# Changing the order of the mixer's input projections in a two-layer hybrid encoder

## The chip, the core and the metric

The kernel runs on one NeuronCore of a Trainium2 chip. Five engines take part: TensorE (PE in the profile, with its weight loads as PEld) multiplies 128x128 tiles into PSUM, VectorE (DVE) and ScalarE (ACT) work on tiles, GpSimd (POOL) does a little arithmetic and issues some transfers, and SyncE (SP) issues the rest. Each engine runs its own list of instructions in a fixed order; semaphores make an instruction wait for what it needs from another engine. The metric is the time of one execution on the device in microseconds, median of several runs; lower is better.

## What is computed

The model has two layers on 512 tokens of width 1024, all in float32. The change touches the first half of a layer, the mixer. One projection of the normalized input makes the gate z, the streams x, B, C of the state-space heads, their step sizes, and the queries, keys and values of the attention heads:

```python
h = rms_norm(x, norm1_w[i])
proj = h @ w_in[i]
z, xbc, dt_raw, q, k, v = jnp.split(proj, [Z_END, XBC_END, DT_END, Q_END, K_END], axis=-1)
xbc = jax.nn.silu(depthwise_conv_centered(xbc, conv_w[i], conv_b[i]))   # 7 taps
xs, bm, cm = jnp.split(xbc, [SSM_WIDTH, SSM_WIDTH + BC_WIDTH], axis=-1)
...
y_fwd = ssd_chunked(xs, dt[:, :, 0], a[0], bm, cm)      # 4 chunks of 128, 2 groups of 8 heads
y_bwd = flip(ssd_chunked(flip(xs), flip(dt[:, :, 1]), a[1], flip(bm), flip(cm)))
y_ssm = y_fwd + y_bwd + d_skip[i][:, None] * xs
y_ssm = rms_norm(y_ssm * silu(z), ssm_norm_w[i])         # per group
y_attn = windowed_gqa(q, k, v, attn_sink[i], band_bias)  # 16 heads, 4 key heads, window 128
x = x + concat([y_ssm, y_attn]) @ w_out[i]
...
x = x + (silu(conv3(g)) * u) @ w_down[i]                 # the FFN half, not touched
```

The attention needs q, k and v. The state-space part of a group needs that group's B, C and x after convolution and Silu, and the gate z only at its end.

## The kernel before

**Dense products.** Every weight and activation is split in a high part and a rest, and a product is three matmuls (`mm3`, L263 to L265): high x high, high x rest, rest x high. Weights come in units of 512 KB, loaded by SyncE into `raw`; ScalarE makes the high part `whi` (L155) and VectorE the rest `wlo` (L156). Units are used in the order in which they are listed (L164 to L193); three split units and three raw ones are held. A projection of 256 columns by `g_ws` (L442) is two such units and two steps (a `yield` after each) of 24 matmuls of 512 columns; the gate projection `g_z` (L738) is four steps of 48 matmuls of 256 columns; the output projection `g_out` (L926) is six steps of 24 matmuls for each half.

**Work beside the dense products.** `Side` (L365) holds a list of smaller steps. `side.run(gen, rate)` goes through the steps of a projection, and after each lets `rate` small steps follow (a credit, at most 2). So rates say how many small steps stand beside one dense step. What is listed here is the order in which the program is written; a scheduler then moves instructions a little within each engine's list.

**The small steps.** Attention has 16 items for a layer, one for each key head and block of 128 queries: scores (`attn_scores`, L551: TensorE L564 and L565 into four small PSUM banks, which VectorE frees by L566; Exp on ScalarE L580), transposes (L598) and values (L608), two items later each. The state-space part (`ssd_steps`, L761) has 14 small steps for a group. For each of eight pieces u (4 chunks, two halves of the heads) `build` makes the weights `dd` (ScalarE L815, VectorE L816) and `decay` the factor `em` (VectorE L826 and L830, Exp on ScalarE L831, VectorE L832), which `inner` multiplies on TensorE (L841). `states` (L778: VectorE L783, TensorE L788, VectorE L790) and `outer` (L851: TensorE L858, VectorE L860 to L863) do the rest; the last one multiplies by the gate `sz`. Then come a scale (L869) and the transposes of the result (L878).

**B, C and x.** After their projection a block of 2 x 128 channels goes through `conv` (L352): one ScalarE instruction (L354) and six taps on VectorE (L360) for each 128 channels, then Silu (L682). Transposes on TensorE follow (L694, L729), written after the next projection so that TensorE need not wait for the Silu.

**The order.** In a layer the program is written thus: values and step sizes, keys, queries of key head 0; queries 1 to 3, then B/C, x (two blocks) and z of group 0, with attention's 19 steps beside them; then B/C, x and z of group 1 with the state-space steps of group 0; then the two output halves with the rest of group 0 and those of group 1. Behind that, `mixT` (L913 to L920) splits the attention result (ScalarE L918, VectorE L919), which is the first operand of the output projection.

**Storage.** Nine 8 KB buffers (`act_tile`) hold the split input hT (4), the keys (2), then x and z of the groups, and later the split attention result and the mixer's result. There are four dense PSUM banks (`psd`) and four small ones (`pss`).

Of the kernel before, what the change touches and what calls it, by code (L numbers as in the profile page):

```python
# [14 lines left out]
P = 128  # L15
# [9 lines left out]
X0 = 1024  # L25
# [16 lines left out]
RATE_Q = 1.3  # L42
RATE_XBC = 0.8
RATE_Z = 0.9
RATE_S0 = 1.2
RATE_S1 = 1.3
# [3 lines left out]
def encoder_kernel(  # L50
# [113 lines left out]
    for i in range(DEPTH):  # L164
# [9 lines left out]
        for g in range(NKV):  # L174
            pair(f"q{g}", [(Q0 + 256 * g, 256)])
        for g in range(GROUPS):
            pair(f"bc{g}", [(B0 + P * g, P), (C0 + P * g, P)])
            pair(f"xa{g}", [(X0 + 512 * g, 256)])
            pair(f"xb{g}", [(X0 + 512 * g + 256, 256)])
            for half in range(2):  # L180
                pair(f"z{g}{half}", [(512 * g + 256 * half, 256)])
# [255 lines left out]
    for i in range(DEPTH):  # L437
        side = Side()
        with ExitStack() as mix:
# [230 lines left out]
            side.run(g_q(0), 0)  # L670
            for g in range(1, NKV):
                side.run(g_q(g), RATE_Q)
            side.steps += [lambda: attn_push(None)] * (LAG + 1)


            def g_xbc(g, r):
# [7 lines left out]
                def bc_done(banks):  # L684
                    bT = ep.tile([P, L], F32, tag="xT", name=nm("bT"), bufs=2)
                    cT = ep.tile([P, L], F32, tag="cT", name=nm("cT"), bufs=2)
                    stage(banks, (8 + g, 10 + g), (bT, cT))
                    r.update(bT=bT, cT=cT)

# [23 lines left out]
                yield from g_ws((i, f"bc{g}"), hT, bc_done)  # L713
                xk = act_tile(F32)
                r["xk"] = xk
                turns = [bc_turn]

                def x_done(b, banks):
                    for t in turns:
                        t()  # L720
                    turns.clear()
# [12 lines left out]
                for b, nme in enumerate(("xa", "xb")):  # L734
                    yield from g_ws((i, f"{nme}{g}"), hT, lambda banks, b=b: x_done(b, banks))
                r["turns"] = turns

            def g_z(g, r):  # L738
                sz = act_tile(F32)
                r["sz"] = sz  # L740
                for half in range(2):
                    ws = [take((i, f"z{g}{half}", j)) for j in range(2)]
                    cs = slice(256 * half, 256 * half + 256)
                    for tp in range(2):
# [8 lines left out]
                        if half == 0 and tp == 0:  # L753
                            for turn in r["turns"]:
                                turn()
# [5 lines left out]
            def ssd_steps(sp, g, r):  # L761

                h0 = GH * g
                xk, bk, cT, cbf, cbb, sz = (r[k] for k in ("xk", "bk", "cT", "cbf", "cbb", "sz"))
# [86 lines left out]
                def outer(c):  # L851
# [10 lines left out]
                    V.tensor_tensor(y, y, pys[c], ALU.add)  # L862
                    V.tensor_tensor(sz[:, c], sz[:, c], y, ALU.mult)  # L863
                    S.activation(y, sz[:, c], AF.Square, accum_out=ss[:, c : c + 1])

                def scale():
                    rs = rstd_of(ss, 512, NT)
                    for c in range(NT):
                        S.mul(sz[:, c], sz[:, c], rs[:, c : c + 1])  # L869
                    mixS[g] = (act_tile(), act_tile())  # L870

                def turn(js):
                    oh_, ol_ = mixS[g]
                    for j in js:
# [28 lines left out]
            side.run(g_xbc(0, r0), RATE_XBC)  # L903
            side.run(g_z(0, r0), RATE_Z)
# [6 lines left out]
            side.run(g_xbc(1, r1), RATE_S0)  # L911
            side.run(g_z(1, r1), RATE_S0)
# [31 lines left out]
            for half in range(2):  # L944
                side.run(g_out(half), RATE_S1)
# [127 lines left out]
```

## Time and profile before

| | |
|---|---|
| time, median of 3 runs | 1590.67 us (1590.48 to 1591.53) |
| time of the profiled execution | 1591.11 us |
| span from the first to the last instruction in it | 1589.4 us |
| mean granted TensorE clock, as a share of full speed | 0.983 |
| TensorE busy | 1529.4 us, 96% of the span |
| weight loads busy | 1248.3 us, 79% |
| VectorE busy | 935.4 us, 59% |
| ScalarE busy | 774.0 us, 49% |
| GpSimd busy | 183.6 us, 12% |

The profiled execution took 0.44 us more than the median, of which 1.7 us lie outside the span. A busy TensorE is not one at its best: matmuls overlap, so their number and the distance from one start to the next say how much work a stretch holds, and what the stretch takes beyond that is lost. Busy shares over the whole span say little here, since a layer has stages with different limits; the two layers are alike, about 780 us apart.

### The profile page before, as it was taken

The page shows a single profiled execution, that of the slowest core. Times are in us where ns is not written, and L with a number is a line of the kernel's source. Part 1 is how long each engine was busy: PE and PEld are TensorE (multiplying, and loading weights), DVE is VectorE, ACT ScalarE, POOL GpSimd, SP SyncE. Part 2 cuts the span into 40 slices and gives each one's busy share as a digit, 9 for nine tenths or more (in the row PEclk, how much of TensorE's full clock was granted, in tenths as well). Part 3 has the DMA queues.
Part 4 walks back from the last instruction along what each step waited for, and adds up shares of the span by engine and source line. Part 5 has one row for each costly group of instructions (what it writes and reads, how often), then busy time and mean ns, then how long its engine had stood idle before and what let it go on. Part 6 is the DMA issues. An engine that isn't in the chain of part 4 may idle for free.

```text
span 1589.4 us, 20122 instructions
## 1 busy us (share of the span) xinstructions
PE 1529.4 (96%) x7676; PEld 1248.3 (79%) x7676; DVE 935.4 (59%) x1494; ACT 774.0 (49%) x1372; POOL 183.6 (12%) x226
## 2 busy tenths in 40 slices
PE   5999999799999999999999999997999999999997
PEld 5877878577788888888887788785778888888886
DVE  3677759997554444433366685799965444443333
ACT  4387885743443333322356779765435323332223
POOL 4000012323200000000010000223322000000002
PEclk9999999799999999999999999997999999999999
DMA  8423233453133333222343322445531332233221
GB/s 247 132 74 85 76 93 94 119 160 93 66 107 106 93 93 105 94 93 93 96 133 101 93 62 60 125 94 145 134 106 60 100 106 93 93 98 101 93 93 66
DMA packets 113796, 162.00 MB, mean 102 GB/s; under 512 B 8010, under 2 KB 90186, under 8 KB 113692
## 3 DMA queue, kind: packets, MB, share of 16 engines
q1 hardware_dynamic: 105476, 133.12, 27.1%
q0 software_dynamic: 7648, 27.50, 7.3%
q8 instruction: 60, 0.98, 0.3%
q14 instruction: 36, 0.29, 0.1%
q10 hardware_dynamic: 576, 0.10, 0.0%
HBM read 156.34 MB, written 8.55 MB: 104 GB/s over the span
## 4 chain that ended last, share of the span: by engine, by line
PE 85%; DVE 7%; ACT 3%; issue 2%; POOL 1%; DMA 1%; POOLq 0%; ACTq 0%; DVEq 0%
PE pd L265 21%; PE pd L263 21%; PE pd L264 21%; PE psm L263 3%; PE psm L264 3%; PE psm L265 3%; PE psm L608 2%; PE psm L598 2%; DVE wlo L156 2%; PE psm L841 2%; PE psm L564 1%; ACT whi L155 1%; PE psm L858 1%; PE psm L565 1%; DVE dd L816 1%
## 5 line engine op out<-in xcount | busy, mean ns | idle before, releaser
L156 DVE TENSOR_TENSOR wlo<-raw,whi 128x1024 fp32r<-128x1024 f32 (+1 forms) x230 | 283.9, 1237 | 279.7 <-ACT whi L155 279.0
L263 PE MATMUL pd<-t,whi 128*128 128x512 f32 (+1 forms) x1088 | 419.6, 386 | 0.0
L265 PE MATMUL pd<-t,wlo 128*128 128x512 f32 (+1 forms) x1088 | 418.5, 385 | 0.4 <-DVE wlo L156 0.4
L264 PE MATMUL pd<-t,whi 128*128 128x512 f32 (+1 forms) x1088 | 417.5, 384 | 0.0
L155 ACT CAST whi<-raw 128x1024 fp32r<-128x1024 f32 (+1 forms) x230 | 238.5, 1041 | 268.7 <-PE pd L264 212.7
L265 PEld LDWEIGHTS pd<-t,wlo 128*128 128x128 f32 x1088 | 204.4, 188 | 41.9 <-DVE wlo L156 1.6
L263 PEld LDWEIGHTS pd<-t,whi 128*128 128x128 f32 x1088 | 204.1, 188 | 40.4 <-issue 2.2
L264 PEld LDWEIGHTS pd<-t,whi 128*128 128x128 f32 x1088 | 204.4, 188 | 39.2 <-issue 1.0
L263 PE MATMUL pd<-whi,t 128*128 128x256 f32 (+2 forms) x544 | 188.7, 347 | 0.6 <-ACT t L756 0.3
L265 PE MATMUL pd<-whi,t 128*128 128x256 f32 (+2 forms) x544 | 183.2, 339 | 2.8 <-DVE t L919 2.8
L264 PE MATMUL pd<-wlo,t 128*128 128x256 f32 (+2 forms) x544 | 182.3, 335 | 0.1
L265 PEld LDWEIGHTS pd<-whi,t 128*128 128x128 f32 x544 | 105.0, 194 | 15.4 <-DVE t L919 5.9
L263 PEld LDWEIGHTS pd<-whi,t 128*128 128x128 f32 x544 | 105.0, 193 | 13.9 <-issue 2.0
L264 PEld LDWEIGHTS pd<-wlo,t 128*128 128x128 f32 x544 | 104.8, 193 | 12.0 <-issue 2.9
L1016 DVE TENSOR_TENSOR pl<-t,ph 128x512 fp32r<-128x512 f32 x40 | 27.7, 692 | 119.4 <-ACT ph L1015 119.4
L1015 ACT CAST ph<-t 128x512 fp32r<-128x512 f32 x40 | 24.8, 620 | 147.7 <-PE psm L264 137.2
L566 DVE CUSTOM_DVE_ANT_0 s<-psm,bias,sink_all 128x256 f32<-128x256 f32 (+1 forms) x128 | 65.9, 547 | 31.4 <-PE psm L565 17.7
L360 DVE SCALAR_TENSOR_TENSOR sg<-pd,fprm,sg 128x511 f32<-128x511 f32 x88 | 65.8, 748 | 30.7 <-ACT sg L354 29.0
L580 ACT ACTIVATE s<-s,nm 128x257 f32<-128x257 f32 (+1 forms) x128 | 70.6, 554 | 13.8 <-DVE nm L577 13.5
L263 PE MATMUL pd<-whi,ph 128*128 128x512 f32 x176 | 69.7, 396 | 0.0
L264 PE MATMUL pd<-wlo,ph 128*128 128x512 f32 x176 | 69.6, 396 | 0.0
L265 PE MATMUL pd<-whi,pl 128*128 128x512 f32 x176 | 69.5, 395 | 0.0
(185 smaller groups left out, 2207.5 us busy)
## 6 DMA issues: line engine op xcount, KB each, us to landing
raw<-in_w_up_dram SPq DMA_DIRECT2D x88, 512.0 KB, 3.5
raw<-in_w_in_dram SPq DMA_DIRECT2D x52, 512.0 KB, 4.1
raw<-in_w_down_dram SPq DMA_DIRECT2D x44, 512.0 KB, 3.5
rows<-sums POOLq DMA_DIRECT2D x32, 512.0 KB, 5.6
raw<-in_w_out_dram SPq DMA_DIRECT2D x32, 512.0 KB, 3.7
bias<-toep POOLq DMA_DIRECT2D x16, 384.0 KB, 4.1
raw<-in_w_in_dram SPq DMA_DIRECT2D x18, 256.0 KB, 3.4
toep<-table POOLq DMA_DIRECT2D x4, 1024.0 KB, 9.4
```

The lines of the kernel that those rows point to most:

```text
L155: S.copy(hi[:, :used], raw[:, :used])
L156: V.tensor_tensor(lo[:, :used], raw[:, :used], f(hi[:, :used]), ALU.subtract)
L263: mm(o, lh, rh, start=start, stop=False)
L264: mm(o, lh, rl, start=False, stop=False)
L265: mm(o, ll, rh, start=False, stop=stop)
L360: V.scalar_tensor_tensor(dst[:, lo:hi], src[:, lo + d : hi + d], taps[k], dst[:, lo:hi], ALU.mult, ALU.add)
L566: V.tensor_tensor_reduce(out=s4[:, h, :w], in0=ps[:, :w], in1=it.bias[h // 2][:, h % 2, it.j0 : it.j1], scale=1.0, scalar=sink4[:, h : h + 1],
L580: S.activation(s4[:, h, : w + 1], s4[:, h, : w + 1], AF.Exp, bias=nm4[:, h : h + 1], accum_out=den[:, h : h + 1])
L598: turn128(ps[:, c : c + P], it.s4[:, h, b * P : (b + 1) * P], ident)
L608: mm(po[c * HD : (c + 1) * HD, :256], v_sb[:, it.k0 // P + b, it.g * HD : (it.g + 1) * HD], it.pts[b][:, c * 256 : (c + 1) * 256], start=( ...
L841: mm(pys[c][:, hc : hc + HD], ems[u][:, h * P : (h + 1) * P], xk[:, c, hc : hc + HD], start=True, stop=True,)
L1016: V.tensor_tensor(l, p_sb[kt], f(h), ALU.subtract)
```

## The change

The list of weight units and the program's order are changed; no operation is added or removed in the program. Group 0's B/C come before the queries; the two x blocks of group 0, B/C of group 1 and both x blocks of group 1 alternate with queries 1 to 3, and all of them but the first two projections run beside attention (rate 1.2). Both gates z now run beside the state-space steps of group 0, before the output projection (rate 1.4 for all of these). The transposes of a convolved block are kept in one list, `turns`, and written after the next projection of B, C, x or z. The state-space steps look up the gate `sz` when they need it, since it is made beside them.

```diff
-RATE_Q = 1.3
-RATE_XBC = 0.8
-RATE_Z = 0.9
-RATE_S0 = 1.2
-RATE_S1 = 1.3
+RATE_A = 1.2
+RATE_S = 1.4
...
         pair("k", [(K0, 256)])
-        for g in range(NKV):
-            pair(f"q{g}", [(Q0 + 256 * g, 256)])
+        for nme in ("bc0", "q0", "xa0", "q1", "xb0", "q2", "bc1", "q3", "xa1", "xb1"):
+            g = int(nme[-1])
...
-            side.run(g_q(0), 0)
-            for g in range(1, NKV):
-                side.run(g_q(g), RATE_Q)
-            side.steps += [lambda: attn_push(None)] * (LAG + 1)
+            turns = []
+            def flush():
+                while turns:
+                    turns.pop(0)()
...
+                return [g_ws((i, f"bc{g}"), hT, bc_first)] + [
+                    g_ws((i, f"{nme}{g}"), hT, lambda banks, b=b: x_done(b, banks)) for b, nme in enumerate(("xa", "xb"))
+                ]
...
-                        if half == 0 and tp == 0:
-                            for turn in r["turns"]:
-                                turn()
+                        flush()
...
             r0, r1 = {}, {}
-            side.run(g_xbc(0, r0), RATE_XBC)
-            side.run(g_z(0, r0), RATE_Z)
+            xs0, xs1 = xbc(0, r0), xbc(1, r1)
+            dense = [xs0[0], g_q(0), xs0[1], g_q(1), xs0[2], g_q(2), xs1[0], g_q(3), xs1[1], xs1[2]]
+            for n, gen in enumerate(dense):
+                side.run(gen, RATE_A if n > 1 else 0)
+                if n == 7:
+                    side.steps += [lambda: attn_push(None)] * (LAG + 1)
+            flush()
             side.finish()
             apx.close()
...
             side.steps += ssd_steps(sp, 0, r0)
-            side.run(g_xbc(1, r1), RATE_S0)
-            side.run(g_z(1, r1), RATE_S0)
+            side.run(g_z(0, r0), RATE_S)
+            side.run(g_z(1, r1), RATE_S)
...
             for half in range(2):
-                side.run(g_out(half), RATE_S1)
+                side.run(g_out(half), RATE_S)
```

How instructions then stand in each engine's list is shown at three places, for layer 0. Each row is line, operation, written tile <- read tiles, columns; x4 means four in a row. In the changed kernel the lines of the state-space part are two higher (L828 is L826 of before), the split of a weight is L153, and that of the attention result L929.

VectorE before, in the middle of group 0's state-space steps: `y` and `t` are the end of chunk 0 (L862, L863), `xT` are taps of the convolution of group 1's second x block, `wlo` weights, `em` and `dd` decay and weights of the next pieces.

```order
L862 TENSOR_TENSOR y_2643<-y_2643,psm_2567 128x512
L360 SCALAR_TENSOR_TENSOR xT_2704<-pd_2586,cprm,xT_2704 128x509
L863 TENSOR_TENSOR t_343_1806<-t_343_1806,y_2643 128x512
L360 SCALAR_TENSOR_TENSOR xT_2704<-pd_2586,cprm,xT_2704 128x510
L360 SCALAR_TENSOR_TENSOR xT_2705<-pd_2587,cprm,xT_2705 128x509
L360 SCALAR_TENSOR_TENSOR xT_2704<-pd_2586,cprm,xT_2704 128x511
L156 TENSOR_TENSOR wlo_2786<-raw_2666,whi_2785 128x1024
L360 SCALAR_TENSOR_TENSOR xT_2704<-pd_2586,cprm,xT_2704 128x511
L156 TENSOR_TENSOR wlo_2958<-raw_2783,whi_2957 128x1024
```

VectorE in the changed kernel from the same place, the end of chunk 0:

```order
L864 TENSOR_TENSOR y_2715<-y_2715,psm_2621 128x512
L832 TENSOR_TENSOR em_2742<-rows_2605 128x512
L866 TENSOR_TENSOR t_459_2389<-t_459_2389,y_2715 128x512
L818 SCALAR_TENSOR_TENSOR dd_2746<-cbb_859,dts_277,dd_2746 128x128 x4
L828 TENSOR_TENSOR rows_2690<-rows_2690,run_276 128x1024
L834 TENSOR_TENSOR em_2742<-em_2742,dd_2725 128x512
L832 TENSOR_TENSOR em_2825<-rows_2690 128x512
L862 TENSOR_TENSOR yo_2833<-psm_2831,ex_278 128x512
```

The taps are gone from this place. Between the first convolution that belongs to it and the first row that splits the attention result, VectorE's list held 36 taps before and holds 12 now; 2 masks are gone (L705), 6 weight splits stand there for 9, 36 of the `dd` rows for 32, 8 of L832 for 7, and 5 of L860 for 6.

TensorE before, at the last pieces of group 0 (`em` are the pieces 4 to 7; `pd` with `t_555` is the output projection, whose first operand is the split attention result):

```order
L841 MATMUL psm_2855<-t_271_1452,em_2750 128x64 x4
L858 MATMUL psm_2935<-st_2555,cT_1374 128x512
L858 MATMUL psm_2940<-st_2469,cT_1374 128x512
L263 MATMUL pd_3125<-whi_2957,t_555_3093 128x512
L264 MATMUL pd_3125<-wlo_2958,t_555_3093 128x512
L841 MATMUL psm_2855<-t_271_1452,em_2861 128x64 x4
L841 MATMUL psm_3019<-t_271_1452,em_2929 128x64 x4
L858 MATMUL psm_3085<-st_2622,cT_1374 128x512
L265 MATMUL pd_3122<-whi_2957,t_556_3094 128x512
L263 MATMUL pd_3122<-whi_2957,t_555_3093 128x512
L264 MATMUL pd_3122<-wlo_2958,t_555_3093 128x512
L841 MATMUL psm_3019<-t_271_1452,em_3025 128x64 x4
```

TensorE in the changed kernel at piece 5, with the gate projection of group 1 around it:

```order
L265 MATMUL pd_2936<-whi_2762,t_12_119 128x256
L843 MATMUL psm_2905<-t_125_867,em_2911 128x64 x4
L860 MATMUL psm_2997<-st_2609,cT_660 128x512
L860 MATMUL psm_3002<-st_2525,cT_660 128x512
L263 MATMUL pd_3029<-whi_2756,t_9_116 128x256
L264 MATMUL pd_3029<-wlo_2757,t_9_116 128x256
L265 MATMUL pd_3029<-whi_2756,t_10_117 128x256
```

Before, the gate projection was used up when piece 4 came, and at most two matmuls of a dense product, or three behind piece 6, stood between the last pieces. Now 48 gate matmuls of 256 columns stand between one piece and the next for pieces 0 to 5, except 11 between 1 and 2 and 37 between 2 and 3; 13 stand before piece 6 and 35 before piece 7.

VectorE before, near the end of attention, beside the gate projection of group 0 (L566 takes a score bank, L584 and L589 end a softmax):

```order
L584 RECIPROCAL rd_2156<-den_2151 128x4
L589 TENSOR_SCALAR s_397_2131<-s_397_2131,rd_2156 128x384 x2
L566 ISA s_414_2240,m_413_2239<-psm_2242,bias_1196,sink_all 128x256
L566 ISA m_413_2239 128x1
L566 ISA s_414_2240,m_413_2239<-psm_2246,bias_1196,sink_all 128x256
```

VectorE in the changed kernel near the end of attention, beside x of group 1 (`xT`), with the masks of group 1 (`cbf`):

```order
L566 ISA s_396_2068,m_395_2067<-psm_2082,bias_1898,sink_all 128x384
L566 ISA m_395_2067 128x1
L360 SCALAR_TENSOR_TENSOR xT_2146<-pd_2015,cprm,xT_2146 128x509
L153 TENSOR_TENSOR wlo_2226<-raw_2021,whi_2225 128x1024
L584 RECIPROCAL rd_2009<-den_2004 128x4
L577 TENSOR_SCALAR nm_401_2086<-m_395_2067 128x4
L709 TENSOR_TENSOR cbf_2136<-psm_2138,t_le 128x512
L589 TENSOR_SCALAR s_377_1984<-s_377_1984,rd_2009 128x384 x2
```

The taps and masks that left the state-space steps stand between attention's rows. ScalarE's list has 54 table loads where it had 48; between the first and the last Exp of attention there are 9 in layer 0 and 11 in layer 1, where there were 12 in each.

## Rows read from the trace of the kernel before

**Rows 1.** Who TensorE waited for: us in total, times, longest.
```profile
PE psm L841 <- DVE em L832: 18.9, 6, 4.9
...
PE psm L878 <- ACT t L869: 6.0, 4, 2.1
...
PE pd L265 <- DVE t L919: 2.8, 2, 1.4
...
PE psm L564 <- ACT x L615: 0.5, 2, 0.3
```

**Rows 2.** Windows: length, busy us (instructions) by engine, TensorE clock, DMA share, GB/s.
```profile
85.00:238.00 153.00, 152.69 (x945) 123.30 (x943) 104.35 (x258) 130.50 (x285) 10.95 (x24) 1.00 0.30 82
...
230.00:290.00 60.00, 59.99 (x365) 51.01 (x362) 58.51 (x90) 40.83 (x70) 12.16 (x11) 1.00 0.38 97
290.00:347.00 57.00, 46.90 (x189) 35.62 (x187) 53.64 (x84) 34.12 (x68) 18.34 (x17) 0.79 0.56 146
```

**Rows 3.** Windows of 4 us in layer 0, columns as above.
```profile
296.00:300.00 4.00, 4.00 (x11) 2.77 (x12) 4.00 (x7) 3.97 (x9) 0.27 (x1) 0.50 0.75 226
...
324.00:328.00 4.00, 4.00 (x23) 3.17 (x22) 3.42 (x8) 3.44 (x6) 0.00 (x0) 1.00 0.27 82
```

**Rows 4.** Timeline of TensorE, both layers: start us, length, engine, line, tile, [wait before].
```profile
228.38 0.65 PE L608 MATMUL psm<-pt,v 128*64 128x256 f32 x4
...
295.89 1.97 PE L841 MATMUL psm<-t,em 128*128 128x64 f32 x8 [2.86 <-DVE em L832]
...
309.16 1.97 PE L841 MATMUL psm<-t,em 128*128 128x64 f32 x8 [3.35 <-DVE em L832]
...
314.32 0.80 PE L265 MATMUL pd<-whi,t 128*128 128x512 f32 x1 [1.38 <-DVE t L919]
...
347.01 1.88 PE L788 MATMUL psm<-xf,bk 128*128 128x512 f32 x4
...
1007.81 0.65 PE L608 MATMUL psm<-pt,v 128*64 128x256 f32 x4
...
1125.90 1.88 PE L788 MATMUL psm<-xf,bk 128*128 128x512 f32 x4
```

**Rows 5.** Timeline of TensorE where it waits for nothing: 512 columns, then 256.
```profile
559.92 0.39 PE L263 MATMUL pd<-t,whi 128*128 128x512 f32 x1
560.15 0.39 PE L264 MATMUL pd<-t,whi 128*128 128x512 f32 x1
...
276.39 0.28 PE L263 MATMUL pd<-whi,t 128*128 128x256 f32 x1
276.51 0.28 PE L264 MATMUL pd<-wlo,t 128*128 128x256 f32 x1
```

**Rows 6.** Timeline of VectorE, layer 0, from the first tap on group 1's B/C.
```profile
227.97 1.53 DVE L360 SCALAR_TENSOR_TENSOR bT<-pd,cprm,bT 128x509 f32<-128x509 f32 x2 [2.69 <-ACT bT L354]
...
249.01 4.01 DVE L360 SCALAR_TENSOR_TENSOR xT<-pd,cprm,xT 128x510 f32<-128x510 f32 x6
...
313.58 0.68 DVE L919 TENSOR_TENSOR t<-x,t 128x512 fp32r<-128x512 f32 x1
```

**Rows 7.** VectorE from 238 to 345 us by line: busy us, mean ns, idle before.
```profile
L816 DVE SCALAR_TENSOR_TENSOR dd<-cbb,dts,dd 128x128 f32<-128x128 f32 x44 | 18.0, 450 | 0.0
...
L156 DVE TENSOR_TENSOR wlo<-raw,whi 128x1024 fp32r<-128x1024 f32 x12 | 15.8, 1314 | 3.2 <-ACT whi L155 3.1
```

**Rows 8.** ScalarE from 85 to 238 us by line, columns as in rows 7.
```profile
L580 ACT ACT_TABLE_LOAD x6 | 7.7, 1283 | 1.8 <-DVE nm L577 1.8
...
L682 ACT ACT_TABLE_LOAD x4 | 5.1, 1283 | 3.1 <-DVE xT L360 2.8 <-DVE bT L360 0.3
L756 ACT ACT_TABLE_LOAD x3 | 3.8, 1283 | 0.1
...
L354 ACT ACTIVATE xT<-pd,cprm 128x512 f32<-128x512 f32 x4 | 3.1, 775 | 0.0
L682 ACT ACTIVATE xT<-xT 128x512 f32<-128x512 f32 x4 | 2.5, 634 | 0.0
```

More of the change, by code (lines that the diff above doesn't have):

```diff
@@ L173, in encoder_kernel @@
         pair("k", [(K0, 256)])
-        for g in range(NKV):
-            pair(f"q{g}", [(Q0 + 256 * g, 256)])
+        for nme in ("bc0", "q0", "xa0", "q1", "xb0", "q2", "bc1", "q3", "xa1", "xb1"):
+            g = int(nme[-1])
+            if nme[0] == "q":
+                pair(nme, [(Q0 + 256 * g, 256)])
+            elif nme[0] == "b":
+                pair(nme, [(B0 + P * g, P), (C0 + P * g, P)])
+            else:
+                pair(nme, [(X0 + 512 * g + 256 * (nme[1] == "b"), 256)])
         for g in range(GROUPS):
-            pair(f"bc{g}", [(B0 + P * g, P), (C0 + P * g, P)])
-            pair(f"xa{g}", [(X0 + 512 * g, 256)])
-            pair(f"xb{g}", [(X0 + 512 * g + 256, 256)])
             for half in range(2):
@@ L668, in g_q, with xbc @@
                 yield from g_ws((i, f"q{g}"), hT, done)
-            side.run(g_q(0), 0)
-            for g in range(1, NKV):
-                side.run(g_q(g), RATE_Q)
-            side.steps += [lambda: attn_push(None)] * (LAG + 1)
-            def g_xbc(g, r):
+            turns = []
+            def flush():
+                while turns:
+                    turns.pop(0)()
+            def xbc(g, r):
                 def stage(banks, cts, dsts):
@@ L688, in bc_done @@
                     r.update(bT=bT, cT=cT)
+                    turns.append(bc_turn)
                 def bc_turn():
@@ L711, in bc_turn @@
                     r.update(bk=bk, cbf=cbf, cbb=cbb)
[L713 to L716, printed above, removed]
                 def x_done(b, banks):
-                    for t in turns:
-                        t()
-                    turns.clear()
+                    flush()
+                    if b == 0:
+                        r["xk"] = act_tile(F32)
+                    xk = r["xk"]
                     xTs = [ep.tile([P, L], F32, tag="xT", name=nm("xT"), bufs=2) for _ in range(2)]
@@ L732, in x_done, with bc_first @@
                         turns.append(turn)
-                for b, nme in enumerate(("xa", "xb")):
-                    yield from g_ws((i, f"{nme}{g}"), hT, lambda banks, b=b: x_done(b, banks))
-                r["turns"] = turns
+                def bc_first(banks):
+                    flush()
+                    bc_done(banks)
+                return [g_ws((i, f"bc{g}"), hT, bc_first)] + [
+                    g_ws((i, f"{nme}{g}"), hT, lambda banks, b=b: x_done(b, banks)) for b, nme in enumerate(("xa", "xb"))
+                ]
             def g_z(g, r):
@@ L752, in g_z @@
                                 mm3(o, ah[:, kt % 4, sl], al[:, kt % 4, sl], hv, lv, kt == 0, kt == KT - 1)
-                        if half == 0 and tp == 0:
-                            for turn in r["turns"]:
-                                turn()
+                        flush()
                         S.activation(sz[:, 2 * tp : 2 * tp + 2, cs], bank.rearrange("p (t c) -> p t c", t=2), AF.Silu)
@@ L763, in ssd_steps @@
                 h0 = GH * g
-                xk, bk, cT, cbf, cbb, sz = (r[k] for k in ("xk", "bk", "cT", "cbf", "cbb", "sz"))
+                xk, bk, cT, cbf, cbb = (r[k] for k in ("xk", "bk", "cT", "cbf", "cbb"))
                 def s2(tag, bufs):
@@ L862, in outer @@
                     V.tensor_tensor(y, y, pys[c], ALU.add)
+                    sz = r["sz"]
                     V.tensor_tensor(sz[:, c], sz[:, c], y, ALU.mult)
@@ L867, in scale @@
                     rs = rstd_of(ss, 512, NT)
+                    sz = r["sz"]
                     for c in range(NT):
@@ L873, in turn @@
                     oh_, ol_ = mixS[g]
+                    sz = r["sz"]
                     for j in js:
@@ L902, in encoder_kernel @@
             r0, r1 = {}, {}
-            side.run(g_xbc(0, r0), RATE_XBC)
-            side.run(g_z(0, r0), RATE_Z)
+            xs0, xs1 = xbc(0, r0), xbc(1, r1)
[4 more added lines that the diff above has]
+                    side.steps += [lambda: attn_push(None)] * (LAG + 1)
+            flush()
             side.finish()
```

## The prediction, made before the changed kernel ran

> **What bounds the kernel now.** I read the busy shares first: TensorE is busy for 96% of the span, so time can only come from the places where it waits or runs at a low clock. The waits of TensorE come next [rows 1]: 18.9 us in 6 waits for `em`, the decay factor of the state-space part, are the largest entry, against 0.5 us before attention's scores. The windows say where [rows 2]. In attention (85 to 238 us) TensorE has work throughout, with VectorE busy 104.4 and ScalarE 130.5 of 153 us. From 230 to 290 us VectorE is full, 58.5 of 60 us, while TensorE still runs. From 290 to 347 us VectorE stays full, TensorE is busy only 46.9 of 57 us, and its clock averages 0.79. [...] So in the stretch where the state-space steps of group 0 stand, VectorE sets the pace, and TensorE pays twice: by waiting, and by running slowly between the waits.
>
> How much the stretch loses is found by counting. I measure from the last attention product (228.4 us) to the first state product of group 1 (347.0) [rows 4]: 118.6 us. In TensorE's list there stand 225 matmuls of 512 columns, 192 of 256, 20 groups of state-space products and some 40 small transposes and products. Where nothing is waited for, a 512-column matmul starts 0.23 us after the one before, a 256-column one 0.12 us [rows 5]; a state product takes 1.88/2 = 0.9 us, and I take 0.9 for each group. So 225 x 0.227 + 192 x 0.12 + 20 x 0.87 + about 5 = 97 us. Lost: 21.5 us. In layer 1 the same stretch runs from 1007.8 to 1125.9, 118.1 us, and loses 21. Together 42.6 us.
>
> VectorE gives the same size independently. Its first tap on group 1's B/C starts at 228.0, its first split of the attention result at 313.6 [rows 6]: 85.6 us, nearly all busy. TensorE's work in that piece of its list is 107 x 0.227 + 192 x 0.12 + 13 x 0.87 + about 6.5 = 65 us. The difference, 20.6, is what TensorE loses, since the output projection behind it needs that split, and waits 1.38 us for it [rows 4].
>
> **What the change does to this stretch.** 24 of the 36 taps leave it. Six taps in a row take 4.01 us [rows 6], so 24 x 0.67 = 16.0 us go. Two masks go (0.68 each, as the split in [rows 6]: 1.4), and three weight splits (1.3 each [rows 7]: 3.9). Four more `dd` rows come in (0.41, somewhat under the mean of 0.45 [rows 7], since neighbours overlap: 1.6), and one row more of L832 against one less of L860: nothing. VectorE's 85.6 become 85.6 - 16.0 - 1.4 - 3.9 + 1.6 = 66 us. Some waiting comes in, because with less to do VectorE now stands for data: the second unit of a gate half can be split only when a held unit is free, shortly before TensorE needs it. That happens at three half changes; the first costs most, since VectorE then has nothing else in front of it. The list put side by side gives about 4 us. So VectorE needs about 70 us.
>
> TensorE's work in the new stretch, from the last x projection to the first output matmul, is 8 x 48 x 0.12 = 46.1, 20 state-space groups at 0.87 = 17.4, and the rest of attention and the last transposes, 5: 68.5 us. The gate matmuls are spread between the pieces, where before the last four pieces stood close together (the two orders of TensorE). VectorE at 70 against TensorE at 68.5 is a near balance. I leave 3 us a layer for it: 1.5 of lateness and as much for a short time at the low clock. From below it can be 0; from above 15, if for each of the eight pieces a table load and the Exp stood uncovered in VectorE's way, 8 x (1.28 + 0.63) [rows 8].
>
> **What it adds to attention.** The work moved must be done there. TensorE's dense work beside attention hardly changes: 12 x 24 x 0.227 + 4 x 48 x 0.12 = 88 us before, 16 x 24 x 0.227 = 87 now. VectorE's list gets one to two blocks of twelve taps more, 8 to 16 us, on 104 of 153. ScalarE gets up to two blocks (each 2 x 0.78 + 2 x 0.63 [rows 8], and two copies of some 0.6: 4.0) and loses four gate Silus of 0.6 and one to four table loads of 1.28: 130.5 + 8 - 2.4 - 3 = 133 of 153. Both stay below TensorE, as ScalarE does now at 85% with 0.5 us of score waits in both layers [rows 1]. The bounds are 0 and what the slow rival below gives; I take 1.5 us a layer, because taps come at every second projection and now stand between the rows that free score banks.
>
> Nothing is gained behind the stretch. The scale at the end of the second group still stands behind the last output matmuls, and the waits for it (6.0 us [rows 1]) stay. The loads keep their number and size. The first queries come one projection later, which delays attention but not TensorE, since B/C fills the place.
>
> **Sum.** 1591.1 - 42.6 + 2 x (3 + 1.5) = 1557.5 for the profiled execution; the median was 0.4 lower, so 1557.
>
> **Rivals.** *The stretch stays late.* Only the taps' arithmetic is sure; `decay` is a chain over three engines, in which VectorE forms the exponent, ScalarE loads a table (the gate's Silu and the decay's Exp alternate) and does the Exp, and VectorE multiplies. If ScalarE, with casts and `dd` rows in its queue, delays each piece, 8 to 15 us of the 21 remain, 12 in the middle: 1591.1 - 42.6 + 2 x (12 + 1.5) = 1575.5. For it speaks that gates now run beside all of these steps, against it that ScalarE has room (34.1 of 57 us [rows 2]) and that 48 gate matmuls, 5.8 us, stand between most pieces. A table load takes 1.28 us [rows 8], and the change puts 54 in the program for 48, 7.7 us of ScalarE. [...]
>
> *The stall moves into attention; slower.* An item's scores fill four banks, freed by VectorE in order. If a block's twelve taps (8.0 us) stand ahead of the freeing row, TensorE stops at the next score. There are ten such blocks in the two layers. With 3 us left in each state-space stretch, the gain is 36.6 us; it is gone from 3.7 us a block on, and at 4.5 us the time is 1591.1 - 36.6 + 45 = 1599.5. Against it: three blocks a layer stand beside attention already, at 0.5 us in all, and the order shows taps and bank rows mixed, not twelve taps in a row. A fall of the clock behind such waits, as at 296 us [rows 3], would make it worse.
>
> *Everything is regained.* VectorE keeps ahead, attention loses nothing: 1591.1 - 42.6 = 1548.5.
>
> *It comes out even.* The rate of 1.4 lets the pieces of group 0 come as fast as VectorE can do them at best, and what is gained is lost at gates and in attention: 1588 to 1594.
>
> **How the numbers follow.** The forecast (1550 to 1567) gets 0.55, a late stretch (1567 to 1585) 0.20, everything regained 0.13, slower 0.07, even 0.05. The range of 1546 to 1580 takes in the first, the third and most of the second, and leaves out some 0.18: slower, even, and the slow end of a late stretch. Faster by over 0.2%, which is about what a measurement of this kernel can tell from no change (3.2 us), holds in the first three cases: 0.88; slower 0.08; the same 0.04.
>
> **What would show it.** Right: waits for `em` fall from 18.9 us to under 5; VectorE is no longer full from 230 to 347 us, but fuller before; the clock keeps 1.00 there; the distance from the last x projection to the first output matmul is near 70 us; the 6.0 us for the scale stay. Wrong: waits for `em` of 2 us and more that come between gate matmuls, with ScalarE as what VectorE waited for, mean the late stretch; waits at L564 for VectorE mean that the stall moved; waits of gate matmuls for `wlo` would mean that I priced the change of halves too low.

## The result and the profile after

The changed kernel takes 1574.82 us (median of 4 runs, 1572.24 to 1575.4) against 1591.03 for the kernel before beside it: a ratio of 0.9894, 95% interval 0.9882 to 0.9906, 16.2 us faster. The forecast was 1557, a gain of 34. The range held the result, at its slow end, but not quite half of the forecast gain came. The profiled execution took 1572.24 us; its terms are set against the 1591.11 us of the profiled execution before.

First the waits of TensorE in the changed kernel (us in total, times, longest). The lines of the state-space part now have numbers higher by 2, by 4 near the scale.

```profile
PE psm L883 <- ACT t L873: 7.9, 11, 2.1
PE psm L843 <- DVE em L834: 7.3, 6, 1.7
...
PE psm L790 <- DVE xf L785: 2.4, 2, 1.8
...
PE psm L790 <- ACT em L833: 1.4, 1, 1.4
PE psm L564 <- DVE m L566: 1.2, 2, 0.8
PE psm L608 <- DVE m L566: 1.1, 1, 1.1
```

Against [rows 1], waits for `em` fall from 18.9 to 7.3 us, forecast "under 5"; waits for `xf` hardly change in sum (2.4 us, 2.2 before), but one of 1.8 us stands where the longest was 0.8. The wait of 2.8 us for the split of the attention result is gone. Attention loses 2.3 us in three waits (L564 and L608) where it lost 0.7, of which [rows 1] shows 0.5.

The windows of layer 0, columns as in [rows 2]:

```profile
240.00:260.00 20.00, 18.18 (x116) 14.26 (x116) 16.11 (x23) 16.34 (x32) 7.62 (x7) 0.91 0.31 80
260.00:280.00 20.00, 19.18 (x134) 16.23 (x134) 18.73 (x33) 13.04 (x22) 8.34 (x6) 1.00 0.57 128
280.00:300.00 20.00, 17.89 (x138) 16.36 (x136) 20.00 (x28) 14.68 (x30) 9.80 (x9) 1.00 0.56 136
300.00:320.00 20.00, 19.24 (x98) 16.13 (x97) 19.88 (x29) 12.47 (x23) 7.35 (x8) 0.91 0.67 208
320.00:340.00 20.00, 19.72 (x91) 15.87 (x91) 19.32 (x35) 13.83 (x26) 2.17 (x3) 1.00 0.65 160
```

The granted clock averages 0.97 in these 100 us, with 0.91 in two of the windows; it averaged 0.79 in 57 us [rows 2]. But VectorE, the third column of busy time, is still full from 280 to 340 us, and TensorE idles 5.8 us in these 100.

The timeline of TensorE gives the ends of the stretch in both layers, the last attention products and the first state product of group 1, and between them, for layer 0, the first matmul of the output projection (`pd<-whi,t` with 512 columns):

```profile
242.82 1.08 PE L608 MATMUL psm<-pt,v 128*64 128x256 f32 x8
...
307.08 0.79 PE L263 MATMUL pd<-whi,t 128*128 128x512 f32 x1
...
338.42 1.88 PE L790 MATMUL psm<-xf,bk 128*128 128x512 f32 x4
...
1015.76 1.08 PE L608 MATMUL psm<-pt,v 128*64 128x256 f32 x8
...
1108.06 1.88 PE L790 MATMUL psm<-xf,bk 128*128 128x512 f32 x4
```

In its list there stand, in layer 0, 120 matmuls of 512 columns, 306 of 256 and 20 state-space groups, which with the small ones is 84.0 us by the prices of the prediction; in layer 1, 29 gate matmuls fewer, 80.5 us. It takes 95.6 and 92.3. So it still loses 11.6 and 11.8 us, where the kernel before lost 21.5 and 21, and where 3 were forecast. Waits are 5.6 us of it in layer 0 and 6.9 in layer 1; behind them the clock stands at 0.50 for some 6.8 us a layer, which by estimate is another 3.4. The last x projection ends at 229 us, so the first output matmul comes 78 us behind it, where the prediction wanted "near 70". So 19.1 us are regained and 17.4 that the forecast counted on are not, which is the size of the miss: 17.8 us by the medians, 14.7 by the profiled executions.

The timeline of VectorE shows where the rows ran long. First the ends that the prediction named, then the middle:

```profile
232.84 7.98 DVE L360 SCALAR_TENSOR_TENSOR xT<-pd,cprm,xT 128x509 f32<-128x509 f32 x12 [1.41 <-PE psm L598]
...
275.82 1.14 DVE L818 SCALAR_TENSOR_TENSOR dd<-cbb,dts,dd 128x128 f32<-128x128 f32 x4
...
280.40 3.86 DVE L818 SCALAR_TENSOR_TENSOR dd<-cbb,dts,dd 128x128 f32<-128x128 f32 x4
...
297.55 1.39 DVE L834 TENSOR_TENSOR em<-em,dd 128x512 f32<-128x512 f32 x1
298.87 1.76 DVE L832 TENSOR_TENSOR em<-rows 128x512 f32<-128x512 f32 x1
...
304.38 1.90 DVE L929 TENSOR_TENSOR t<-x,t 128x512 fp32r<-128x512 f32 x3
```

Four `dd` rows take 1.14 us at 275.82 and 3.86 at 280.40; the two `em` rows take 1.39 and 1.76, where such rows take 0.68 elsewhere. At the same times GpSimd works (its timeline):

```profile
276.83 3.37 POOL L855 TENSOR_TENSOR y<-t,skip_all 128x512 f32<-128x512 f32 x1 [0.51 <-ACT y L867]
...
280.91 2.67 POOL L863 TENSOR_TENSOR y<-y,yo 128x512 f32<-128x512 f32 x2
...
297.13 2.94 POOL L863 TENSOR_TENSOR y<-y,yo 128x512 f32<-128x512 f32 x2 [1.57 <-DVE yo L862]
```

Both sides are slow: the product at 276.83 takes 3.37 us, and 1.13 us at 302.99. These are GpSimd's rows of `outer`: the product with `d_skip` (L855) and the adding of `yo` to `y` (L863).

VectorE also waits for GpSimd, at the row that reads the finished `y` (us in total, times, longest; 5.8 us in the kernel before):

```profile
DVE y L864 <- POOL y L863: 6.6, 5, 2.2
```

### The profile page after: what moved, and what is told of

Its sections match the earlier page's. It is cut to its first block, busy times and chain, and to the rows that moved or that the text cites. A ratio compares the mean times of both kernels' runs of the same rounds, so it can differ in the third digit from the quotient of the medians.

```text
span 1570.5 us, 20117 instructions
## 1 busy us (share of the span) xinstructions
PE 1518.9 (97%) x7676; PEld 1242.4 (79%) x7676; DVE 936.9 (60%) x1494; ACT 780.1 (50%) x1378; POOL 186.3 (12%) x226
## 4 chain that ended last, share of the span: by engine, by line
PE 81%; DVE 9%; issue 3%; ACT 3%; POOL 2%; DMA 1%; POOLq 0%; DVEq 0%; ACTq 0%
PE pd L263 21%; PE pd L264 20%; PE pd L265 20%; PE psm L263 3%; PE psm L264 3%; PE psm L265 3%; PE psm L608 2%; PE psm L598 2%; DVE dd L818 2%; DVE wlo L153 2%; PE psm L564 1%; ACT whi L152 1%; PE psm L565 1%; DVE rows L828 1%; PE psm L843 1%
## 5 line engine op out<-in xcount | busy, mean ns | idle before, releaser
L153 DVE TENSOR_TENSOR wlo<-raw,whi 128x1024 fp32r<-128x1024 f32 (+1 forms) x230 | 282.1, 1230 | 267.6 <-ACT whi L152 266.2
L263 PEld LDWEIGHTS pd<-whi,t 128*128 128x128 f32 x544 | 106.2, 195 | 13.7 <-issue 3.3
L360 DVE SCALAR_TENSOR_TENSOR sg<-pd,fprm,sg 128x511 f32<-128x511 f32 x88 | 65.9, 749 | 30.7 <-ACT sg L354 29.0
L566 DVE CUSTOM_DVE_ANT_0 s<-psm,bias,sink_all 128x256 f32<-128x256 f32 (+1 forms) x128 | 65.5, 548 | 22.8 <-PE psm L565 10.3
L360 DVE SCALAR_TENSOR_TENSOR xT<-pd,cprm,xT 128x511 f32<-128x511 f32 (+2 forms) x96 | 66.9, 743 | 5.8 <-ACT xT L354 3.8
```

Of the source, the lines that this page charges most:

```text
L153: V.tensor_tensor(lo[:, :used], raw[:, :used], f(hi[:, :used]), ALU.subtract)
L263: mm(o, lh, rh, start=start, stop=False)
L360: V.scalar_tensor_tensor(dst[:, lo:hi], src[:, lo + d : hi + d], taps[k], dst[:, lo:hi], ALU.mult, ALU.add)
L566: V.tensor_tensor_reduce(out=s4[:, h, :w], in0=ps[:, :w], in1=it.bias[h // 2][:, h % 2, it.j0 : it.j1], scale=1.0, scalar=sink4[:, h : h + 1],
```

## The experiments

Three theories stood against each other. **ScalarE** (the prediction's slow rival): its table loads and Exp delay each piece. **VectorE's volume**: it simply has more rows than the stretch has time for. **GpSimd**: its rows hold up VectorE's, either because the two engines get in each other's way at SBUF (contention) or because VectorE waits for what GpSimd makes (dependency). Medians are given, with the ratio to the kernel before and its 95% interval.

**1. No Silu at the gate.**

```diff
-S.activation(sz[:, 2 * tp : 2 * tp + 2, cs], ..., AF.Silu)
+S.activation(sz[:, 2 * tp : 2 * tp + 2, cs], ..., AF.Copy)
```

> The changed kernel with Copy in place of the Silu of the gate, a function that needs no table load (the Silu is left out of the result): of the 54 table loads 22 go, about ten from the stretch of each layer in which the state-space steps stand beside the gates. Three theories say why that stretch still loses about 11 us a layer. ScalarE theory (the slow rival of the prediction: load and Exp delay each piece): 14 to 20 us go, 1555 to 1561. VectorE theory (VectorE is full from 260 to 360 us, ScalarE only waits for it): 0 to 4 us, 1571 to 1576. GpSimd theory (VectorE's rows are longer while GpSimd works): 0 to 4 us as well.

Measured: 1573.15 us, 0.9889 (0.9874 to 0.9903). Indistinguishable from the changed kernel. ScalarE's table loads ahead of the decay's Exp nearly vanish, first row of the changed kernel, second of this one:

```profile
L833 ACT ACT_TABLE_LOAD x13 | 16.7, 1283 | 0.2
```

```profile
L833 ACT ACT_TABLE_LOAD x2 | 2.6, 1283 | 0.0
```

Of the 54 loads 32 are left, none of them at the gate, where there were 13. So some 28 us of loads (22 by 1.28) lay beside other work. The ScalarE theory falls, as far as it rests on the loads. The Exp was not taken out, but VectorE's rows behind it waited 0.8 us for it in all (L834, first rows of run 3).

**2. No taps on the last x block of group 1.**

```diff
 for k in range(nt):
     d = k - half
-    if d == 0:
+    if d == 0 or notaps:
         continue
...
```

> The changed kernel without the twelve taps of the last x block of group 1 (left out of the result): VectorE has 8 us a layer less to do, right ahead of the first steps of group 0, and nothing else changes. VectorE theory: most of the 16 us comes back as time, 10 to 16 us, 1559 to 1565. ScalarE theory: the pieces still wait for load and Exp, 0 to 4 us, 1571 to 1576. GpSimd theory: the rows behind are as long as before, but start earlier, 8 to 16 us; this run does not tell it from the VectorE theory.

Measured: 1571.18 us, 0.9878 (0.9863 to 0.9892): 3.6 us for 16 us of VectorE rows. The waits for `em` are no longer among TensorE's seven largest, but others came up in their place:

```profile
PE psm L885 <- ACT t L875: 10.2, 11, 2.1
...
PE pd L264 <- DVE wlo L153: 3.9, 3, 2.0
PE psm L862 <- DVE st L794: 3.5, 2, 1.8
```

and VectorE waits for the first `dd` in layer 0 (8.0 us in layer 1), since ScalarE's part stands behind the last attention copies:

```profile
238.21 2.17 DVE L820 SCALAR_TENSOR_TENSOR dd<-cbb,dts,dd 128x128 f32<-128x128 f32 x7 [6.50 <-ACT dd L819]
```

So of the 8 us a layer that were freed, VectorE spent 6.5 and 8.0 waiting. Room ahead of the steps is worth little, and what I expected of both theories here was too high; but since VectorE could not use the room, the run says little against its volume.

**3. GpSimd's part of `outer` left out.**

```diff
-G.tensor_tensor(v3(y), v3(xk[:, c]), bc_last(skip_all[...], HD), ALU.mult)
 for d in range(2):
     ...
-    G.tensor_tensor(y, y, yo, ALU.add)
+    y = yo
 V.tensor_tensor(y, y, pys[c], ALU.add)
```

> The changed kernel without GpSimd's part of outer (the product with d_skip and the adding of yo are left out of the result; VectorE and TensorE keep their rows): GpSimd keeps only the products for st. GpSimd theory: the VectorE rows that took 1.2 to 2.7 us more beside GpSimd, together some 8 us in the stretch of layer 0, take their usual time, and 8 to 16 us go, 1559 to 1567. VectorE theory without contention, and ScalarE theory: the sum of VectorE's rows is the same, 0 to 3 us, 1572 to 1576.

Measured: 1553.36 us, 0.9764 (0.975 to 0.9779): 21 us, more than any theory had. The rows of VectorE by line, first in the changed kernel, then here (busy us, mean ns, idle before):

```profile
L818 DVE SCALAR_TENSOR_TENSOR dd<-cbb,dts,dd 128x128 f32<-128x128 f32 x128 | 57.5, 494 | 3.2 <-ACT dd L817 3.2
L832 DVE TENSOR_TENSOR em<-rows 128x512 f32<-128x512 f32 x32 | 26.9, 841 | 1.3 <-PE psm L843 1.3
L834 DVE TENSOR_TENSOR em<-em,dd 128x512 f32<-128x512 f32 x32 | 25.1, 783 | 1.0 <-ACT em L833 0.8
L862 DVE TENSOR_TENSOR yo<-psm,ex 128x512 f32<-128x512 f32 x24 | 15.9, 683 | 0.2
```

```profile
L818 DVE SCALAR_TENSOR_TENSOR dd<-cbb,dts,dd 128x128 f32<-128x128 f32 x128 | 43.8, 382 | 3.2 <-ACT dd L817 3.2
L832 DVE TENSOR_TENSOR em<-rows 128x512 f32<-128x512 f32 x32 | 22.6, 706 | 4.7 <-PE psm L843 4.6
L834 DVE TENSOR_TENSOR em<-em,dd 128x512 f32<-128x512 f32 x32 | 21.9, 683 | 0.7 <-ACT em L833 0.3
...
L860 DVE TENSOR_TENSOR yo<-psm,ex 128x512 f32<-128x512 f32 x24 | 16.0, 684 | 0.7 <-PE psm L858 0.5
```

The same number of rows takes 13.7 + 4.3 + 3.2 = 21.2 us less; all of VectorE is 27.5 us less busy (936.9 to 909.4), with as many rows, so their number is not what costs. The wait of 6.6 us for `y` goes too, so this run alone does not tell contention from dependency. The row for `yo`, with one operand in PSUM, keeps its 0.68 us. TensorE's stretch, measured as above, takes 86.9 us for 84.0 of work in layer 0 and 82.2 for 80.5 in layer 1: lost, 2.9 and 1.7, as the prediction wanted.

**4. Rates 1.1 and 1.7.**

```diff
-RATE_S = 1.4
+RATE_S = 1.1
+RATE_O = 1.7
...
-side.run(g_out(half), RATE_S)
+side.run(g_out(half), RATE_O)
```

> The changed kernel with the steps at 1.1 a piece beside the gates and 1.7 beside the output projection, instead of 1.4 beside both: nothing is left out, the same rows stand in another order, with fewer steps in the stretch where VectorE is full and more where it idles (380 to 400 us). VectorE theory: 4 to 10 us go, 1565 to 1571. ScalarE theory: the same number of loads alternate, 0 to 3 us, 1572 to 1576. Against both: slower by 2 to 8 us if the output projection of the first half now waits for the steps of group 0.

Measured: 1571.15 us, 0.9881 (0.9863 to 0.9899): 3.7 us by the medians, and the interval reaches that of the changed kernel. Inconclusive.

**5. Contention or dependency: products on a scratch tile.** Run 3, with as many products and sums on GpSimd that nobody reads.

```diff
-y = s2("y", 2)
+u = s2("y", 2)
-G.tensor_tensor(v3(y), v3(xk[:, c]), bc_last(skip_all[...], HD), ALU.mult)
+G.tensor_tensor(v3(u), v3(xk[:, c]), bc_last(skip_all[...], HD), ALU.mult)
 ...
-    G.tensor_tensor(y, y, yo, ALU.add)
+    G.tensor_tensor(u, u, u, ALU.add)
+    y = yo
```

> As the run without GpSimd's part of outer (1553 us), but GpSimd does as many products and sums of the same shape on a scratch tile that nobody reads (the results stay out, as there). Contention theory (VectorE's rows with two operands in SBUF stand still while GpSimd works): most of the 21 us comes back, 1566 to 1576. Dependency theory (VectorE and TensorE waited for y, which GpSimd made): it stays at 1551 to 1557.

Measured: 1590.02 us, 1.0001 (0.9991 to 1.0011). Not 21 but 37 us come back, though nobody waits for these rows. With nothing to wait for, they run in a block. VectorE's timeline (the last of the three `dd` rows is shown once more by itself), then GpSimd's, then TensorE's:

```profile
250.95 1.53 DVE L832 TENSOR_TENSOR em<-rows 128x512 f32<-128x512 f32 x1
252.41 8.90 DVE L818 SCALAR_TENSOR_TENSOR dd<-cbb,dts,dd 128x128 f32<-128x128 f32 x3
261.23 1.28 DVE L785 TENSOR_TENSOR xf<-t,sd 128x512 f32<-128x512 f32 x2
...
254.50 6.81 DVE L818 SCALAR_TENSOR_TENSOR dd<-cbb,dts,dd 128x128 f32<-128x128 f32 x1
```

```profile
255.14 1.05 POOL L863 TENSOR_TENSOR y<-y 128x512 f32<-128x512 f32 x1
256.14 1.05 POOL L855 TENSOR_TENSOR y<-t,skip_all 128x512 f32<-128x512 f32 x1
257.14 2.03 POOL L863 TENSOR_TENSOR y<-y 128x512 f32<-128x512 f32 x2
...
260.13 1.03 POOL L863 TENSOR_TENSOR y<-y 128x512 f32<-128x512 f32 x1
```

```profile
261.97 3.78 PE L790 MATMUL psm<-xf,bk 128*128 128x512 f32 x4 [9.08 <-DVE xf L785]
```

Three `dd` rows (0.86 us at ease) take 8.90, and end just after the last row of GpSimd's block; TensorE stands 9.08 us for the `xf` behind them. VectorE's rows are long while they run, not while they wait, and nothing waits for the scratch rows. That is contention. It is not a measure of its size in the changed kernel, since there the rows lie apart.

**6. The kernel before without GpSimd's part**, the edit of run 3 made on the kernel before.

> The kernel before without GpSimd's part of outer (left out of the result as in that run): it asks whether the kernel before paid for GpSimd too. The dd, em and rows lines of VectorE took 16 us more there than in the changed kernel without GpSimd's part. If VectorE sets the pace there, as the prediction has it, 14 to 25 us go: 1566 to 1577. If contention is new with the change: 0 to 5 us, 1586 to 1591.

Measured: 1584.05 us, 0.9962 (0.9948 to 0.9977): 6.6 us. Neither guess. GpSimd's part cost the kernel before a third of what it costs the changed one. Without that part the change is worth 1584.05 - 1553.36 = 30.7 us; with it, 16.2.

**7 and 8. Moving the work of `outer` off GpSimd, one part each**, nothing left out. First the adding on VectorE, then the product on ScalarE:

```diff
-    G.tensor_tensor(y, y, yo, ALU.add)
+    V.tensor_tensor(y, y, yo, ALU.add)
```

```diff
-G.tensor_tensor(v3(y), v3(xk[:, c]), bc_last(skip_all[...], HD), ALU.mult)
+for h in range(GH):
+    hs = slice(h * HD, (h + 1) * HD)
+    S.mul(y[:, hs], xk[:, c, hs], skip_all[:, 16 * i + h0 + h : 16 * i + h0 + h + 1])
```

> The changed kernel with the adding of yo on VectorE instead of GpSimd; nothing is left out. VectorE gets 24 rows of 0.68 more, 16 us, and loses what 35 of GpSimd's 60 us of outer cost it, about 13 us. Contention theory: about even with the changed kernel, 1571 to 1578. Dependency theory (the wait for y through two engines costs): 5 to 10 us faster, 1565 to 1570. VectorE volume theory (only VectorE's sum counts, GpSimd costs it nothing): 10 to 16 us slower, 1585 to 1591.

> The changed kernel with the product with d_skip on ScalarE, eight rows of 64 columns for each, instead of one row on GpSimd; nothing is left out. GpSimd loses 25 of its 60 us of outer, ScalarE gets 128 rows, some 12 to 15 us a layer on about 110 of 175. Contention theory: 5 to 10 us go, 1565 to 1570, as ScalarE has room. ScalarE theory (its queue delays each piece): 5 us slower or more, 1580 to 1590. Dependency theory: even, 1572 to 1577.

Measured: 1572.59 us, 0.9893 (0.9875 to 0.9911), and 1568.07 us, 0.9863 (0.9848 to 0.9878). Both inside what contention gave: 16 us of VectorE rows cost nothing where contention goes, and 34 us of ScalarE rows cost less than 25 us of GpSimd rows. They also bear on the dependency in the changed kernel. In run 7 VectorE's wait for `y` is gone and VectorE is about as busy as in the changed kernel (934.8 against 936.9 us), and only 2.2 us go, less than can be told from nothing. In run 8 that wait grows to 11.5 us, and the kernel is 6.8 us faster.

**9. The same number of GpSimd rows that read nothing.** Run 5 with a fill for each product and sum.

```diff
-G.tensor_tensor(u, u, u, ALU.add)
+G.memset(u, 0.0)
```

> The run with scratch products (1590 us) with a fill of the same size in place of each product and sum: GpSimd has 40 rows at the same places of its list, but they read nothing. If VectorE's rows stand still because both engines read operands from SBUF, it falls back to about the run without GpSimd's part, 1551 to 1560. If GpSimd being busy, its writes, or the loads queued behind its rows cost the time, it stays at 1575 to 1592.

Measured: 1551.07 us, 0.9751 (0.9737 to 0.9766), the same as with no rows at all. GpSimd's and VectorE's lines here:

```profile
L864 POOL MEMSET y<- 128x512 f32 x24 | 12.5, 537 | 0.0
L855 POOL MEMSET y<- 128x512 f32 x16 | 8.6, 535 | 0.0
```

```profile
L818 DVE SCALAR_TENSOR_TENSOR dd<-cbb,dts,dd 128x128 f32<-128x128 f32 x128 | 43.8, 382 | 3.2 <-ACT dd L817 3.2
```

40 rows that write 128x512 leave `dd` at 382 ns, as run 3 has it; with the products of run 5 its mean was 504. So GpSimd's rows that read operands from SBUF cost VectorE time, and rows of the same number that only write cost nothing that these runs can tell. Both stand in this run side by side: three `dd` rows beside fills take 0.86 us (at 250.95), four beside the products for `st`, which read, 2.92 for 1.14 (at 256.47). The fills are half as long as the products (0.54 us for 1.03), so a load queued behind them is held up less; but in run 5 VectorE waited for no load in the stretch of layer 0, its rows ran long.

**10 and 11. Both parts off GpSimd; and the product on ScalarE with rates 1.2 and 1.6.** The edits of 7 and 8 together; the edit of 8 with that of 4 at other numbers. Nothing left out.

> The changed kernel with the d_skip product on ScalarE and the adding of yo on VectorE; nothing is left out, and GpSimd keeps only the products for st. Contention theory: the 21 us that GpSimd's part costs come back less some of the 16 us of VectorE rows and of the 17 us a layer of ScalarE rows, 1560 to 1568. Volume theory (VectorE full at any rate): 1570 to 1578. ScalarE theory: 1570 or more.

> The changed kernel with the d_skip product on ScalarE (1568 us) and the steps at 1.2 a piece beside the gates and 1.6 beside the output projection; nothing is left out. If the two gains are of different causes (contention, and VectorE's crowding beside the gates), 2 to 5 us more go, 1563 to 1566. If the rates only move the waits, 1567 to 1572.

Measured: 1568.56 us, 0.9863 (0.9847 to 0.9879), and 1555.26 us, 0.9778 (0.9763 to 0.9792). Run 10 lies just above what contention gave: at rate 1.4 the second part brings nothing on top of the first. In run 11 the rates bring 13 us, more than I gave them.

**12 and 13. The rates alone; and both parts off GpSimd with the rates.** What was open, as it was put on record: whether the rate is a cause of its own.

> The changed kernel with the steps at 1.2 a piece beside the gates and 1.6 beside the output projection, and GpSimd's part of outer left where it is; nothing is left out. The d_skip product on ScalarE gave 7 us, the same with these rates 13 us more. If the rates alone bring the 13 us (VectorE's crowding beside the gates), 1559 to 1564. If they bring them only once GpSimd does less, 1568 to 1576, as the rates 1.1 and 1.7 did.

> The d_skip product on ScalarE, the adding of yo on VectorE (1569 us), and the rates 1.2 and 1.6; nothing is left out. If GpSimd's contention is what is left, it is the fastest of all with its whole part of outer gone from GpSimd, 1549 to 1555. If VectorE's added rows weigh as much as the contention that goes, as they did at 1.4, even with the run that leaves the adding on GpSimd, 1553 to 1558.

Measured: 1566.04 us, 0.9851 (0.9837 to 0.9866): the rates alone bring 8.8, between the two guesses. And 1547.69 us, 0.9735 (0.9719 to 0.9751), the fastest of all, 27 us below the changed kernel with the whole computation in it. TensorE's waits with the rates alone:

```profile
PE psm L884 <- ACT t L874: 8.5, 2, 4.5
PE pd L266 <- DVE t L930: 4.5, 3, 2.5
...
PE psm L844 <- DVE em L835: 2.3, 3, 1.7
```

The waits for `em` are fewer, but one of up to 4.5 us stands in each layer at the scale, and others at the attention split. The stretch that the prediction was about takes longer with the rates alone, 99.1 and 94.4 us against 95.6 and 92.3. What they gain lies behind it, at the end of the output projection. VectorE's timeline there, first in the changed kernel, then with the rates alone, from the last row of the two output halves (L951, L952) to the first of the part that needs group 1's result (L981, L982):

```profile
394.75 0.69 DVE L951 TENSOR_TENSOR x<-x,pd 128x512 f32<-128x512 f32 x1 [0.36 <-PE pd L265]
...
410.65 0.69 DVE L981 TENSOR_TENSOR x<-x,pd 128x512 f32<-128x512 f32 x1 [0.82 <-PE pd L265]
```

```profile
396.44 1.88 DVE L952 TENSOR_TENSOR x<-x,pd 128x512 f32<-128x512 f32 x3
...
407.75 0.69 DVE L982 TENSOR_TENSOR x<-x,pd 128x512 f32<-128x512 f32 x1 [0.83 <-PE pd L266]
```

The starts of these two rows lie 15.9 us apart in the changed kernel (14.9 in layer 1) and 10.1 in both layers with the rates, where the last of the three rows starts at 397.64: group 1's scale now starts ahead of that row and not behind it. In the kernel before they lay 15.7 and 15.5 us apart. So this gain is not part of what the forecast missed. In run 13 both places are better: the stretch takes 87.8 and 84.3 us, the end 10.6 twice.

| | GpSimd does `outer` | product on ScalarE | and adding on VectorE |
|---|---|---|---|
| rate 1.4 | 1574.8 | 1568.1 | 1568.6 |
| rates 1.2, 1.6 | 1566.0 | 1555.3 | 1547.7 |

The two measures are worth 8.8 and 6.3 us apart, and 27.1 together. Each alone gives part of its gain back at the other place: with both parts moved at rate 1.4 (run 10) the stretch falls to 90.1 and 88.1 us, but the end grows to 17.1 in both layers, which takes back 3.4 of the 9.7 us that the stretch gains; and the rates alone lengthen the stretch by 5.6.

## Why the prediction was right or wrong

**Right: where the loss was, and which rows leave.** VectorE was to need 66 us and some 4 of waiting from its first tap to the first split of the attention result; it needed 71.5 (232.84 to 304.38), 66.3 of them busy, after the 85.6 of [rows 6]. That busy time came out in spite of rows that GpSimd made long, since the sum started from a list in which they were long already. The waiting came at the first `dd` (2.64 us), not at the weights of a half gate, for which TensorE waited 0.6 us in all. The clock fell less (0.97 from 230 to 347 us, 0.90 before), but did not keep 1.00.

**Right: attention and what lies behind.** Attention's new waits, 2.3 against 0.7 us, are 0.8 a layer, forecast 1.5. The waits for the scale were to stay at 6.0 us and take 7.9.

**Wrong: "I leave 3 us a layer for it".** The near balance of VectorE (70) and TensorE (68.5) was to cost 3 us a layer and cost 11.7. Both sums were near: VectorE took 71.5 us, and TensorE's 78 less 4.7 of waits and 3.4 for the low clock are 70. What failed was to take a balance of sums for a bound on the wait. The list held, between its ends, rows, single or four in a row, that ran 0.7 to 2.7 us longer where GpSimd's product or sum lay beside them, and among those are the `dd` and `em` rows of the very pieces that TensorE waits for. Without GpSimd's part the same order with the same VectorE rows loses 2.9 and 1.7 us (run 3), and the kernel takes 1553.4, or 1551.1 with the fills: the forecast, 1557, had priced that kernel.

The prediction has no term for GpSimd at all: its 18 of 57 us in [rows 2] went unread, and 0.45 us was taken as what a `dd` row costs [rows 7]. That mean was a mixture already, of 0.28 us at ease (1.14 for four) and over a microsecond in contention (one takes 1.17 us at 299.75 in the kernel before, beside a GpSimd product). By runs 5 and 9 the rows of GpSimd that read contend (products 1590.0 us), and those that only write do not (fills 1551.1). On VectorE's side rows that read two operands from SBUF grow, from run 9 to run 5 the mean of `dd` from 382 to 504 ns and that of `xf` from 722 to 1164, while `yo`, one of whose operands is in PSUM, stays at 683 to 685 ns in the changed kernel and in runs 3, 5 and 9. By what means the two engines hold each other up, no run here shows.

**Where the missing gain went.** Of 17.8 us that did not come, GpSimd's part takes 14.5: the change is worth 30.7 us without it (run 3 against run 6) and 16.2 with it. By runs 5 and 7 to 9 most of that is contention; the exact share of VectorE's waits for `y` was not measured. The other 3 are about the uncertainty of this difference, whose two ratios are known to 0.0015 each, 2.4 us. Why the same rows of GpSimd cost only 6.6 us before is argued, not shown. VectorE's rows were not spared there: without GpSimd's part it is 22.3 us less busy (935.4 to 913.1, run 6), against 27.5 in the changed kernel. But the stretch before keeps losing 20 and 18 us of its 21.5 and 21 without that part (run 6, counted as above), so it seems that the last four pieces, which stood close together, lost their time anyway.

**The rivals.** The time came out at the centre of *the stretch stays late*, 1575.5, but not by its mechanism. It had ScalarE's load and Exp in VectorE's way; run 1 takes 22 loads out for 1.7 us, less than can be told from nothing. ScalarE itself waited for VectorE in 19.9 of the 29.6 us that it idled from 240 to 340 us. So the table loads that the change adds (54 for 48), which the prediction named beside this rival, cost nothing here that these runs can tell. *The stall moves into attention* did not happen (0.8 us a layer). *It comes out even* named the rate of 1.4 as a fault, in the stretch. There a lower rate helped nothing by itself; the 8.8 us of run 12 come from the end of the output projection, of which the prediction said rightly that the change gains nothing there.

**What stays open.** Besides the small cost of GpSimd in the kernel before: run 4, with 1.1 and 1.7, leaves the end of the output projection at 15.9 and 14.9 us, and why it does not gain as 1.2 and 1.6 do was not followed. Nor was it tried what such rates would give the kernel before.

## What to carry to other kernels

When two engines' sums in a stretch come out nearly equal, the difference of the sums need not bound the wait: here it followed single rows that ran long in the chain between the two. Look for rows whose single times stray far from their mean before pricing a balance, and look at what the other engines do beside them. GpSimd at 12% busy was not free here: a `dd` row of VectorE, which reads two operands from SBUF, took 6.81 us beside six GpSimd rows that read (run 5), against 0.28 at ease, and fills in their place cost nothing that could be told (run 9). Elementwise work with one scalar for each head was cheaper here as eight ScalarE rows of 0.34 us than as one GpSimd row of 1.59 on average: 6.8 us (run 8). After moving work between stages the rate at which small steps are dealt out is worth setting again: it brought a third of the 27 us that were still to be had, though not in the stretch that the change was about.

## What the runs showed of the hardware

One VectorE row stood through a whole block of GpSimd's rows, not through one: a `dd` row took 6.81 us in run 5 (254.50 to 261.31), while six products and sums of 1.03 to 1.05 us ran back to back. Spread out, the same kind of row cost VectorE 0.7 to 2.7 us at the places shown in the changed kernel (an `em` row 1.39 for 0.68, four `dd` rows 3.86 for 1.14), and GpSimd's own row grew from 1.13 to 3.37 us. A fill of 128x512 took 0.54 us on GpSimd and cost VectorE nothing that these runs can tell (`dd` at 382 ns in run 9 as in run 3), where a product or sum of that size took 1.03 to 1.05 in run 5.
